# A SwiGLU feed-forward network with seven block products moved from the down projection to the up and gate projections

## The chip, the cores and the metric

The program runs on one core of a Trainium2 chip. Its time is the device time of one execution in microseconds (us); the median of three runs is compared. Five engines work side by side, each through its own queue: TensorE (PE: matrix products into PSUM, with its weight loads shown as PEld), VectorE (DVE), ScalarE (ACT), GpSimd (POOL) and SyncE (SP, which here starts most of the transfers).

## The reference

Two layers act on a state h of 512 tokens by 1024 channels, all in float32. Each layer is an RMSNorm, an input projection into four head groups (two kinds of softmax attention, a gated delta rule and a gated linear attention), an output projection, and then the part that matters here, a feed-forward network of width 2816, followed by a gate from a second input:

```
hn = _rmsnorm(h, norm_ffn[l])
h = h + (jax.nn.silu(hn @ w_gate[l]) * (hn @ w_up[l])) @ w_down[l]
gate = jax.nn.sigmoid(_rmsnorm(h, norm_ple[l]) @ w_ple_gate[l])
h = h + gate * (p[l] @ w_ple_proj[l])
```

`_rmsnorm(x, g)` is x divided by the root of the mean of its squares (plus 1e-6), times g. After the two layers one more RMSNorm follows.

## The kernel before

The state is kept transposed: channels on the 128 partitions, 512 tokens along a row, so h is eight tiles `h[0..7]` of 128x512. Every float32 operand of a product is split into a high and a low part in a narrower float format (`hi` by an ACT copy, `lo` by a DVE subtraction), and each product of a 128x128 weight block with a tile is three matmuls, hi by hi, hi by lo and lo by hi (`mm3`, lines 309 to 311, recorded for every product of the kernel).

A plain block (`block`, `gblock`) makes 128 rows of a projection: it loads eight 128x128 weight blocks in two halves of 128x512 (`weights`, lines 278 to 282, from four raw buffers into four pairs of split buffers), and accumulates eight times three matmuls of 512 columns in one of two `acc` banks of PSUM.

`seven` makes a 2x2 block product by seven block products in place of eight (Strassen's scheme in Winograd's form). The fixed side is a 2x2 arrangement of weights: two row blocks of the output by two halves of the depth, `a11, a21, a22, a12`, each 128 x (128 per pair). The moving side is a 2x2 arrangement of two tiles of depth by two halves of 256 tokens, or sums of these made in advance. Each of the seven products is, with four pairs, twelve matmuls of 256 columns; DVE makes the sums of the weights (lines 392, 393, 397 or 403, 418) and, for each of the seven products, ACT and DVE split the fixed side (`fixed_parts`, lines 362 and 363). Four banks of the pools `mixg` and `mixl` take the results.

The feed-forward network of a layer runs in three parts of 8, 8 and 6 of its 22 blocks f (`FF_PARTS`). In every part, for each f, a plain block of gate, a product with R (the reciprocal root of the norm, line 1428), Silu on ACT, a plain block of up, and two products on DVE (lines 1437 and 1438) make a tile u. In parts 0 and 1 two such tiles go through `moving_parts`, which makes the moving side's sums and splits; then four calls of `seven` make the part's share of the eight rows of down and add it to h, and what several results share is collected in `u2` and added by `shared_sums` after part 1. In part 2 the tiles are split plainly, and eight plain down blocks of six products each are added to h (line 1450). A norm comes before (`norm`, which also makes gate block 0) and after.

The order of the work on each engine is made when the program is built: the framework takes instructions in program order where they are ready by its own estimate and where buffers are free, so an instruction can stand ahead of others that come before it in the text. At run time each engine works through its list in that order, and waits on semaphores. A buffer tag holds a fixed number of tiles (`G_BUFS`, `BIG_BUFS`, `RP_BUFS`); whoever asks for one more waits for the first that is let go.

Of the kernel before, what the change touches and what calls it, by code (L numbers as in the profile page):

```python
# [8 lines left out]
F32 = mybir.dt.float32  # L9
# [22 lines left out]
ACC_BUFS = 2  # L32
BIG_BUFS = 5

M_TAGS = (("g",) * 5 + ("e",) * 2, ("g",) * 5 + ("e",) * 2, ("g",) * 4 + ("lg",) * 2 + ("e",), ("g",) * 3 + ("pt",) * 2 + ("o",) * 2)
RP_BUFS = 4
DEPTH = 2
FF = 2816
# [94 lines left out]
def _weights(i):  # L133

    tiles = {}

    def tblock(key, b):
        k = b.shape[0] // P
        t = np.zeros((P, 8, P), np.float32)
        t[:, :k] = b.reshape(k, P, P).transpose(1, 0, 2)  # L140
        tiles[key] = t.reshape(P, D)

    for l in range(DEPTH):
        w = np.asarray(i["w_in"][l])
# [12 lines left out]
        pp = np.asarray(i["w_ple_proj"][l]).reshape(2, P, 2, 4, P)  # L157
        for half in range(2):
            tiles[l, "ple", half] = pp[:, :, half].transpose(1, 2, 0, 3).reshape(P, D)
        w, wp = np.asarray(i["w_out"][l]), np.asarray(i["w_ple_gate"][l])  # L160
        wa = w[:2 * P].reshape(2, P, 2, 4, P)
        for half in range(2):
            tiles[l, "outa", half] = wa[:, :, half].transpose(1, 2, 0, 3).reshape(P, D)
        g, u, dn = (np.asarray(i[n][l]) for n in ("w_gate", "w_up", "w_down"))
        for n in range(KB):
            c = slice(n * P, (n + 1) * P)
            tblock((l, "out", n), w[2 * P:, c])
            tblock((l, "pgate", n), wp[:, c])
            for part, (f0, nf) in enumerate(FF_PARTS):
                d = dn[f0 * P:(f0 + nf) * P, c]  # L170
                if part < 2:

                    d = d.reshape(nf // 2, 2, P, P).transpose(1, 0, 2, 3).reshape(nf * P, P)
                tblock((l, "down", part * KB + n), d)
        for f in range(FB):
            tblock((l, "gate", f), g[:, f * P:(f + 1) * P])
            tblock((l, "up", f), u[:, f * P:(f + 1) * P])
    return np.stack([tiles[k] for k in _TILES])


# [22 lines left out]
class _Trunk:  # L203
# [122 lines left out]
        return ps  # L326


    def moving_parts(self, u, j):

        nc = self.nc
        t = self.gp.tile([P, 2 * T], F32, tag="rp", bufs=RP_BUFS, name=self.name("t"))
        u4, t4 = (a.rearrange("p (a b c) -> p a b c", a=2, b=2) for a in (u, t))

        nc.vector.tensor_sub(t4[:, :, 0, :], u4[:, :, 1, :], u4[:, 0])
        nc.vector.tensor_sub(t4[:, 0, 1, :], u4[:, 1, 1, :], t4[:, 0, 0, :])
        nc.vector.tensor_sub(t4[:, 1, 1, :], u4[:, 1, 0, :], t4[:, 0, 1, :])
        tags = iter(M_TAGS[j])
        tile = lambda: self.g("m", F32R, tag=next(tags))
        first = tile()  # L340
        b11 = first[:, :256], first[:, 256:]
        nc.scalar.activation(b11[0], u4[:, 0, 0, :], AF.Copy)
        nc.vector.tensor_sub(b11[1], u4[:, 0, 0, :], b11[0].bitcast(F32))
        parts = []
        for src in (t[:, :T], t[:, T:], u[:, T:]):
            hi, lo = tile(), tile()
            nc.scalar.activation(hi, src, AF.Copy)
            nc.vector.tensor_sub(lo, src, hi.bitcast(F32))
            parts += [(hi[:, c:c + 256], lo[:, c:c + 256]) for c in (0, 256)]
        return [b11, *parts]  # L350

    def raw(self, name, i, c, n):
        raw = self.wrp.tile([P, HALF], F32, tag="w", name=self.name("w"))
# [9 lines left out]
        nc.vector.tensor_sub(lo, raw, hi.bitcast(F32))  # L363
        return hi, lo

    def seven(self, ms, name, i, h, u2, part):

        nc = self.nc
        n = len(ms) * P
        a11, a21, a22, a12 = (self.raw(name, part * KB + i + r, c * n, n) for r, c in ((0, 0), (1, 0), (1, 1), (0, 1)))

        def product(ps, parts, which, start=True, pairs=range(len(ms))):
            hi, lo = parts
# [8 lines left out]
        left, right = slice(0, 256), slice(256, 512)  # L385
# [3 lines left out]
        early, late = range(len(ms) - (i == 0)), range(len(ms) - (i == 0), len(ms))  # L389
# [6 lines left out]
        if i == 0:  # L396
# [5 lines left out]
        if i:  # L402
            nc.vector.tensor_sub(a21, a11, a21)
            w7 = self.fixed_parts(a21)
        if part == 0:
            nc.scalar.activation(u2, p1, AF.Copy)
        else:
            nc.vector.tensor_add(u2, u2, p1)
# [4 lines left out]
        nc.vector.tensor_add(h[1][:, right], h[1][:, right], p5)  # L413
        product(p1, self.fixed_parts(a12), b21, start=False)
        nc.vector.tensor_add(h[0][:, left], h[0][:, left], p1)
        product(p7, self.fixed_parts(a22), t4, start=False)
        nc.vector.tensor_add(h[1][:, left], h[1][:, left], p7)
        nc.vector.tensor_sub(s2, a12, s2)
        product(p5, self.fixed_parts(s2), b22, start=False)
        nc.vector.tensor_add(h[0][:, right], h[0][:, right], p5)  # L420

    def shared_sums(self, h, u2):

        nc = self.nc
        nc.vector.tensor_add(h[0][:, 256:], h[0][:, 256:], u2)
        h2 = h[1].rearrange("p (a t) -> p a t", a=2)
        nc.vector.tensor_add(h2, h2, u2.unsqueeze(1).to_broadcast([P, 2, 256]))

    def gvproj(self, xs, name):

# [955 lines left out]
    def run(self):  # L1386
# [11 lines left out]
        for l in range(DEPTH):  # L1398
# [13 lines left out]
            self.gt = "gl"  # L1412
            xs, R, ps = self.norm(h, self.v(V_FFN, KB), "gate")
            self.table("silu_and_others")
            for part, (f0, nf) in enumerate(FF_PARTS):
                if part == 2:
                    ph = []
                    for k in range(2):
                        t = self.g("pt")
                        nc.sync.dma_start(t, self.pT[l, k])  # L1420
                        ph.append(self.split(t, "p"))
                ms = []
                if part == 0:
                    u2 = self.gp.tile([P, KB // 2, 256], F32, tag="rp", bufs=RP_BUFS, name=self.name("u2"))
                for f in range(f0, f0 + nf):
                    pg = self.block(xs, "gate", f) if f else ps
                    t, sg = self.g("fg"), self.g("fs")
                    nc.vector.tensor_mul(t, pg, R)  # L1428
                    self.act(sg, t, AF.Silu)
                    pu = self.block(xs, "up", f)  # L1430
                    if part == 2:
                        u = self.g("fu")
                    elif f % 2 == 0:
                        both = self.big("fu")
                    if part < 2:
                        u = both[:, f % 2 * T:(f % 2 + 1) * T]
                    nc.vector.tensor_mul(u, pu, R)  # L1437
                    nc.vector.tensor_mul(u, u, sg)
                    if part == 2:
                        self.gt = "g"  # L1440
                        ms.append(self.split(u, "m"))
                        self.gt = "gl"
                    elif f % 2:
                        ms.append(self.moving_parts(both, len(ms)))
                for n in range(0, KB, 1 if part == 2 else 2):
                    if part < 2:
                        self.seven(ms, "down", n, h[n:n + 2], u2[:, n // 2, :], part)
                        continue
                    ps = self.block(ms, "down", part * KB + n)
                    nc.vector.tensor_add(h[n], h[n], ps)  # L1450
                if part == 1:
                    for n in range(0, KB, 2):
                        self.shared_sums(h[n:n + 2], u2[:, n // 2, :])

            self.gt = "g"
            self.table("natural_log_exp_and_others")
# [107 lines left out]
```

## Time and profile before

| what | before |
|---|---|
| median of 3 runs | 1516.2 us (1514.39 to 1516.46) |
| the profiled execution's own time | 1513.12 us |
| its span, instructions | 1511.3 us, 27858 |
| PE, PEld busy | 1460.5 us (97%), 1220.8 us (81%) |
| DVE, ACT, POOL busy | 1004.9 us (66%), 681.1 us (45%), 113.8 us (8%) |
| mean granted TensorE clock | 0.983 |

The busy shares are means over stages of different kinds. An operation's duration runs from its start to its end and overlaps its successor's, so the pace of a row of like operations is read from start to start. In the views a group's line is that of the helper that issued it: the tile names (`acc` for a plain block, `bank` for `seven`) tell the stages apart.

### The profile page before, as it was taken

The page shows a single profiled execution, that of the slowest core. Times are in us where ns is not written, and L with a number is a line of the kernel's source. Part 1 is how long each engine was busy: PE and PEld are TensorE (multiplying, and loading weights), DVE is VectorE, ACT ScalarE, POOL GpSimd, SP SyncE. Part 2 cuts the span into 40 slices and gives each one's busy share as a digit, 9 for nine tenths or more (in the row PEclk, how much of TensorE's full clock was granted, in tenths as well). Part 3 has the DMA queues.
Part 4 walks back from the last instruction along what each step waited for, and adds up shares of the span by engine and source line. Part 5 has one row for each costly group of instructions (what it writes and reads, how often), then busy time and mean ns, then how long its engine had stood idle before and what let it go on. Part 6 is the DMA issues. An engine that isn't in the chain of part 4 may idle for free.

```text
span 1511.3 us, 27858 instructions
## 1 busy us (share of the span) xinstructions
PE 1460.5 (97%) x10856; PEld 1220.8 (81%) x10856; DVE 1004.9 (66%) x2012; ACT 681.1 (45%) x1298; POOL 113.8 (8%) x174
## 2 busy tenths in 40 slices
PE   8989999999999999999999899899999999999996
PEld 6768787878898889887878788778788988898875
DVE  7757865666585679456687558565765956874654
ACT  7624533544443434344574434344543434343554
POOL 0151020100000000000003401210000000000011
PEclk9999999999999999999999979999999999999998
DMA  5485125423323324323434721362232333243232
GB/s 200 101 227 109 41 67 173 126 81 99 97 89 113 97 78 133 97 82 112 129 105 108 207 72 49 101 184 74 92 97 90 100 105 98 77 133 95 91 95 77
DMA packets 108631, 162.55 MB, mean 108 GB/s; under 512 B 26803, under 2 KB 36436, under 8 KB 108500
## 3 DMA queue, kind: packets, MB, share of 16 engines
q1 hardware_dynamic: 83328, 142.95, 30.1%
q0 software_dynamic: 7872, 14.68, 4.1%
q10 hardware_dynamic: 17300, 3.14, 1.3%
q8 instruction: 86, 1.41, 0.4%
q14 instruction: 45, 0.37, 0.1%
HBM read 141.72 MB, written 19.01 MB: 106 GB/s over the span
## 4 chain that ended last, share of the span: by engine, by line
PE 84%; DVE 6%; issue 3%; DMA 3%; ACT 2%; POOL 2%; ACTq 0%; DVEq 0%; SPq 0%; POOLq 0%
PE acc L309 21%; PE acc L310 20%; PE acc L311 20%; PE bank L309 3%; PE bank L311 3%; PE bank L310 3%; PE mix L624 2%; PE mix L615 1%; PE mix L593 1%; DMA rp<-qk 1%; PE acc L445 1%; PE acc L443 1%; PE mix L1267 1%; DMA nx<-dn 1%; PE acc L444 1%
## 5 line engine op out<-in xcount | busy, mean ns | idle before, releaser
L309 PE MATMUL acc<-y,wh 128*128 128x512 f32 x1320 | 531.5, 403 | 11.8 <-ACT wh L281 7.6
L311 PE MATMUL acc<-y,wl 128*128 128x512 f32 x1320 | 522.8, 396 | 1.7 <-issue 0.9
L310 PE MATMUL acc<-y,wh 128*128 128x512 f32 x1320 | 521.5, 395 | 0.3 <-DVE y L525 0.3
L281 ACT ACTIVATE wh<-w 128x512 fp32r<-128x512 f32 (+1 forms) x404 | 243.2, 604 | 391.8 <-PE acc L310 315.0
L282 DVE TENSOR_TENSOR wl<-w,wh 128x512 fp32r<-128x512 f32 (+1 forms) x404 | 267.8, 664 | 145.7 <-ACT wh L281 144.7
L309 PEld LDWEIGHTS acc<-y,wh 128*128 128x128 f32 x1320 | 251.1, 190 | 72.0 <-ACT wh L281 9.9
L311 PEld LDWEIGHTS acc<-y,wl 128*128 128x128 f32 x1320 | 250.9, 190 | 56.0 <-issue 2.0
L310 PEld LDWEIGHTS acc<-y,wh 128*128 128x128 f32 x1320 | 251.0, 190 | 50.1 <-DVE y L525 2.1
L309 PE MATMUL bank<-m,wh 128*128 128x256 f32 x448 | 126.8, 286 | 2.7 <-ACT wh L362 2.3
L311 PE MATMUL bank<-m,wl 128*128 128x256 f32 x448 | 126.1, 283 | 0.5 <-DVE wl L363 0.5
L310 PE MATMUL bank<-m,wh 128*128 128x256 f32 x448 | 126.4, 283 | 0.0
L309 PEld LDWEIGHTS bank<-m,wh 128*128 128x128 f32 x448 | 85.2, 192 | 5.4 <-ACT wh L362 3.7
L266 ACT ACTIVATE e<-logit,mx 128x128 f32<-128x128 f32 (+3 forms) x96 | 53.5, 557 | 76.2 <-DVE mx L603 73.9
L311 PEld LDWEIGHTS bank<-m,wl 128*128 128x128 f32 x448 | 85.8, 192 | 0.9 <-DVE wl L363 0.9
L310 PEld LDWEIGHTS bank<-m,wh 128*128 128x128 f32 x448 | 85.9, 192 | 0.4
L1437 DVE TENSOR_TENSOR fu<-acc,rstd 128x512 f32<-128x512 f32 x44 | 30.4, 691 | 61.4 <-PE acc L311 61.4
L1428 DVE TENSOR_TENSOR fg<-acc,rstd 128x512 f32<-128x512 f32 x44 | 30.3, 689 | 49.2 <-PE acc L311 46.1
L362 ACT ACTIVATE wh<-s 128x512 fp32r<-128x512 f32 x48 | 30.1, 628 | 64.7 <-DVE s L393 31.8
L624 PEld LDWEIGHTS mix<-vn,pt 128*128 128x128 f32 x320 | 44.8, 195 | 7.2 <-DVE pt L621 1.9
L362 ACT ACTIVATE wh<-w 128x512 fp32r<-128x512 f32 x64 | 40.1, 630 | 21.4 <-PE bank L310 15.1
L624 PE MATMUL mix<-vn,pt 128*128 128x64 f32 x320 | 45.6, 273 | 0.5 <-DVE pt L621 0.3
L363 DVE TENSOR_TENSOR wl<-w,wh 128x512 fp32r<-128x512 f32 x64 | 43.9, 686 | 2.9 <-ACT wh L362 2.1
(320 smaller groups left out, 2079.3 us busy)
## 6 DMA issues: line engine op xcount, KB each, us to landing
w<-wt SPq DMA_DIRECT2D x420, 256.0 KB, 2.6
rp<-qk POOLq DMA_DIRECT2D x32, 256.0 KB, 5.5
qk<-qkh SPq DMA_DIRECT2D x24, 256.0 KB, 4.8
qk<-qkl SPq DMA_DIRECT2D x24, 256.0 KB, 5.2
rp<-qk POOLq DMA_DIRECT2D x12, 512.0 KB, 4.3
w<-wt SPq DMA_DIRECT2D x48, 128.0 KB, 2.2
h<-xT SPq DMA_DIRECT2D x16, 256.0 KB, 4.7
spill<-h SPq DMA_DIRECT2D x8, 256.0 KB, 3.1
```

The lines of the kernel that those rows point to most:

```text
L266: i = self.nc.scalar.activation(out, in_, func, **k).ins
L281: nc.scalar.activation(hi[:, :n], raw[:, :n], AF.Copy)
L282: nc.vector.tensor_sub(lo[:, :n], raw[:, :n], hi[:, :n].bitcast(F32))
L309: nc.tensor.matmul(ps, wh, xh, start=start, stop=False, **how)
L310: nc.tensor.matmul(ps, wh, xl, start=False, stop=False, **how)
L311: nc.tensor.matmul(ps, wl, xh, start=False, stop=stop, **how)
L362: nc.scalar.activation(hi, raw, AF.Copy)
L363: nc.vector.tensor_sub(lo, raw, hi.bitcast(F32))
L443: nc.tensor.matmul(o, xh[:, tok], hi, start=first, stop=False, skip_group_check=True)
L624: nc.tensor.matmul(po, pt[:, kb * P:(kb + 1) * P], v(kb), start=kb == 0, stop=kb == qb, skip_group_check=True)
L1428: nc.vector.tensor_mul(t, pg, R)
L1437: nc.vector.tensor_mul(u, pu, R)
```

## The change

Gate, up and down swap their forms. Up is made by `seven` for all pairs of blocks f but the first (ten units a layer), gate by `seven` for the pairs 8, 10, 12, 14, 16 and 18 (six units); gate pairs 0 to 6 and 20, and up pair 0, stay plain. All of down is made of plain blocks, with the splits of u that these need. The moving side of the new units comes from h itself: `normed_parts` scales four pairs of tiles of h by the gain on ACT, forms the sums on DVE and splits them, once a layer, after the first pair. The plain down blocks of a part no longer stand behind it but in the next part, between its gate and up units: none beside pair 8, then two behind up 8, then one ahead of and one behind each up; in part 2 none beside pair 16, four behind up 16, two ahead of and two behind up 18. The down blocks of part 2 still come last. The results go out through `scaled` (gate, times R) and `gated` (up, times the gate's tile, which is silu(g R) times R). `moving_parts`, `u2` and `shared_sums` are gone.

```diff
+GATES = range(8, 20, 2)
-    def moving_parts(self, u, j):
...
+    def differences(self, u0, u1):
+        a, b = slice(0, 256), slice(256, 512)
+        nc.vector.tensor_sub(u0[:, a], u0[:, b], u0[:, a])
+        nc.vector.tensor_sub(u0[:, b], u1[:, b], u0[:, b])
+        nc.vector.tensor_sub(u1[:, b], u1[:, b], u0[:, a])
+        nc.vector.tensor_sub(u1[:, a], u1[:, a], u1[:, b])
+    def normed_parts(self, h, gain, xs, j):
+        us = [self.g("x", tag="g") for _ in range(2)]
+        for u, x, c in zip(us, h, range(2)):
+            nc.scalar.activation(u, x, AF.Copy, scale=gain[:, c:c + 1])
+        self.differences(*us)
...
+            out += self.parts_of(u, hi, lo)
...
-    def seven(self, ms, name, i, h, u2, part):
+    def seven(self, ms, name, i, take, late_rows=False):
...
-        nc.vector.tensor_add(u2, u2, p6)
-        product(p7, w7, t3, pairs=late if i == 0 else early)
-        nc.vector.tensor_add(h[1][:, right], h[1][:, right], p7)
+        take("1", p1)
+        take("6", p6)
+        product(p7, w7, t3, pairs=late if late_rows else early)
+        take("7", p7)
...
+    def gated(self, u, gates):
+        u2 = self.g("u2", tag="gl")[:, :256]
+        q = [u[:, c:c + 256] for c in range(0, 1024, 256)]
+        def take(what, ps):
+            if what == "1":
+                nc.scalar.activation(u2, ps, AF.Copy)
+            elif what == "6":
+                nc.vector.tensor_add(u2, u2, ps)
+            elif what == "7":
+                nc.vector.tensor_add(q[3], u2, ps)
+            elif what == "5":
+                nc.vector.tensor_add(q[3], q[3], ps)
+            elif what == "11":
+                nc.vector.tensor_mul(q[0], ps, gates[0][:, :256])
+            elif what == "21":
+                nc.vector.tensor_add(q[2], u2, ps)
+                nc.vector.tensor_mul(u[:, T:], u[:, T:], gates[1])
+            else:
+                nc.vector.tensor_add(q[1], u2, ps)
+                nc.vector.tensor_mul(q[1], q[1], gates[0][:, 256:])
...
             for part, (f0, nf) in enumerate(FF_PARTS):
+                split, made = made, []
+                downs = list(range(KB)) if part else []
+                per = 2 if part == 2 else 1
+                for f in range(f0, f0 + nf, 2):
+                    if part == 2 and not downs:
...
+                    if f in GATES:
+                        self.seven(xts, "gate", f, self.scaled(gates, R))
+                    for j, t in enumerate(gates):
+                        if f not in GATES:
+                            nc.vector.tensor_mul(t, self.block(xs, "gate", f + j) if f + j else ps, R)
+                        self.act(t, t, AF.Silu)
+                        nc.vector.tensor_mul(t, t, R)
+                        if f == 0:
+                            nc.vector.tensor_mul(us[j], self.block(xs, "up", j), t)
+                    if split:
+                        ms = [self.split(m[:, c:c + T], "m") for m in split for c in (0, T)]
+                        split = []
+                    elif downs:
+                        for n in downs[:per]:
+                            down(n)
+                        downs = downs[per:]
+                    if f == 0:
+                        xts = [self.normed_parts(h[2 * j:2 * j + 2], self.v(V_FFN + 2 * j, 2), xs[2 * j:2 * j + 2], j)
+                               for j in range(KB // 2)]
+                    else:
+                        self.seven(xts, "up", f, self.gated(both, gates))
+                    made.append(both)
+                    n2 = per + per * (f == f0)
+                    for n in downs[:n2]:
+                        down(n)
+                    downs = downs[n2:]
+            ms += [self.split(m[:, c:c + T], "m") for m in made for c in (0, T)]
+            for n in range(KB):
+                acc = self.block(ms, "down", 2 * KB + n)
+                nc.vector.tensor_add(h[n], h[n], acc)
```

`scaled` is built as `gated` is, with R in place of the gate's tile and one product on 512 columns and two on 256. The order of the weights in memory follows the new forms; their amount is the same.

## Rows read from the trace of the kernel before

**Rows 1.** The page: busy engines, and the chain that ended last by engine.
```profile
PE 1460.5 (97%) x10856; PEld 1220.8 (81%) x10856; DVE 1004.9 (66%) x2012; ACT 681.1 (45%) x1298; POOL 113.8 (8%) x174
...
PE 84%; DVE 6%; issue 3%; DMA 3%; ACT 2%; POOL 2%; ACTq 0%; DVEq 0%; SPq 0%; POOLq 0%
```
**Rows 2.** Windows, layer 0's feed-forward: us, PE, PEld, DVE, ACT, POOL, clock, DMA, GB/s.
```profile
341.00:363.00 22.00, 22.00 (x95) 17.53 (x95) 13.71 (x23) 9.40 (x15) 0.00 (x0) 1.00 0.35 108
363.00:426.70 63.70, 63.70 (x283) 52.76 (x282) 39.24 (x65) 24.93 (x41) 0.00 (x0) 1.00 0.29 91
426.70:467.20 40.50, 40.12 (x327) 39.35 (x326) 37.20 (x70) 19.26 (x35) 0.00 (x0) 1.00 0.32 100
467.20:557.80 90.60, 90.60 (x416) 75.63 (x415) 52.59 (x87) 33.63 (x56) 0.00 (x0) 1.00 0.32 98
557.80:600.00 42.20, 40.97 (x328) 39.84 (x327) 41.37 (x83) 19.21 (x33) 0.00 (x0) 1.00 0.36 111
655.00:688.00 33.00, 33.00 (x147) 27.33 (x146) 20.78 (x34) 17.12 (x30) 0.00 (x0) 1.00 0.31 92
```
**Rows 3.** Timeline of PE, plain blocks: start, duration, engine, line, operation.
```profile
639.61 0.39 PE L309 MATMUL acc<-y,wh 128*128 128x512 f32 x1
639.84 0.39 PE L310 MATMUL acc<-y,wh 128*128 128x512 f32 x1
...
647.09 0.39 PE L309 MATMUL acc<-y,wh 128*128 128x512 f32 x1
```
**Rows 4.** Timeline of PE, inside a unit of seven products.
```profile
449.72 0.28 PE L309 MATMUL bank<-m,wh 128*128 128x256 f32 x1
449.84 0.28 PE L310 MATMUL bank<-m,wh 128*128 128x256 f32 x1
...
452.96 0.28 PE L309 MATMUL bank<-m,wh 128*128 128x256 f32 x1
```
**Rows 5.** Groups by line between 340 and 690 us, with what ended the idle time.
```profile
L309 PE MATMUL bank<-m,wh 128*128 128x256 f32 x224 | 63.4, 286 | 1.3 <-ACT wh L362 1.1
...
L281 ACT ACTIVATE wh<-w 128x512 fp32r<-128x512 f32 (+1 forms) x101 | 62.1, 615 | 112.2 <-PE acc L310 101.0 <-PE bank L310 4.0 <-ACT sq L508 2.9
```
**Rows 6.** Timeline of PE: first matmul of four units, and first behind them.
```profile
426.69 0.28 PE L309 MATMUL bank<-m,wh 128*128 128x256 f32 x1
...
468.44 0.40 PE L309 MATMUL acc<-y,wh 128*128 128x512 f32 x1
...
555.51 0.28 PE L309 MATMUL bank<-m,wh 128*128 128x256 f32 x1
...
598.11 0.40 PE L309 MATMUL acc<-y,wh 128*128 128x512 f32 x1
...
1170.66 0.28 PE L309 MATMUL bank<-m,wh 128*128 128x256 f32 x1
...
1212.40 0.40 PE L309 MATMUL acc<-y,wh 128*128 128x512 f32 x1
...
1299.46 0.28 PE L309 MATMUL bank<-m,wh 128*128 128x256 f32 x1
...
1342.06 0.40 PE L309 MATMUL acc<-y,wh 128*128 128x512 f32 x1
```
**Rows 7.** Timeline of PE, its longest wait in a unit.
```profile
567.92 0.28 PE L311 MATMUL bank<-m,wl 128*128 128x256 f32 x1
568.84 0.39 PE L309 MATMUL bank<-m,wh 128*128 128x256 f32 x1 [0.64 <-ACT wh L362]
```
**Rows 8.** Timeline of DVE inside the units of part 1.
```profile
589.26 0.68 DVE L363 TENSOR_TENSOR wl<-w,wh 128x512 fp32r<-128x512 f32 x1
589.86 0.41 DVE L408 TENSOR_TENSOR u<-u,bank 128x256 f32<-128x256 f32 x1
590.19 0.68 DVE L363 TENSOR_TENSOR wl<-s,wh 128x512 fp32r<-128x512 f32 x1
590.80 0.68 DVE L363 TENSOR_TENSOR wl<-w,wh 128x512 fp32r<-128x512 f32 x1
```
**Rows 9.** Windows of about one unit each, late in part 1 and in part 0.
```profile
578.00:588.00 10.00, 10.00 (x85) 10.00 (x85) 9.74 (x21) 3.75 (x7) 0.00 (x0) 1.00 0.40 133
588.00:598.00 10.00, 10.00 (x86) 10.00 (x85) 9.87 (x21) 5.80 (x10) 0.00 (x0) 1.00 0.42 132
456.00:466.00 10.00, 10.00 (x86) 10.00 (x85) 8.96 (x18) 5.06 (x9) 0.00 (x0) 1.00 0.33 105
```

More of the change, by code (lines that the diff above doesn't have):

```diff
@@ L169, in _weights @@
             for part, (f0, nf) in enumerate(FF_PARTS):
[L170 to L174, printed above, removed]
+                tblock((l, "down", part * KB + n), dn[f0 * P:(f0 + nf) * P, c])
         for f in range(FB):
-            tblock((l, "gate", f), g[:, f * P:(f + 1) * P])
-            tblock((l, "up", f), u[:, f * P:(f + 1) * P])
+            pairs = lambda d: d.reshape(KB // 2, 2, P, P).transpose(1, 0, 2, 3).reshape(D, P)
+            c = slice(f * P, (f + 1) * P)
+            tblock((l, "gate", f), pairs(g[:, c]) if f // 2 * 2 in GATES else g[:, c])
+            tblock((l, "up", f), pairs(u[:, c]) if f > 1 else u[:, c])
     return np.stack([tiles[k] for k in _TILES])
@@ L326, in gblock @@
         return ps
-    def moving_parts(self, u, j):
+    def differences(self, u0, u1):
         nc = self.nc
[L332 to L350, printed above, removed]
+        a, b = slice(0, 256), slice(256, 512)
[3 more added lines that the diff above has]
+        nc.vector.tensor_sub(u1[:, a], u1[:, a], u1[:, b])
@@ new lines, in parts_of @@
+    def parts_of(self, src, hi, lo):
+        nc = self.nc
+        nc.scalar.activation(hi, src, AF.Copy)
+        nc.vector.tensor_sub(lo, src, hi.bitcast(F32))
+        return [(hi[:, c:c + 256], lo[:, c:c + 256]) for c in range(0, src.shape[1], 256)]
+    def normed_parts(self, h, gain, xs, j):
+        nc = self.nc
+        us = [self.g("x", tag="g") for _ in range(2)]
+        for u, x, c in zip(us, h, range(2)):
+            nc.scalar.activation(u, x, AF.Copy, scale=gain[:, c:c + 1])
+        self.differences(*us)
+        tags = iter(X_TAGS[j])
+        out = []
+        for u in us:
+            tag = next(tags)
+            if tag == "rp":
+                p = self.gp.tile([P, 2, T], F32R, tag="rp", bufs=RP_BUFS, name=self.name("xt"))
+                hi, lo = p[:, 0, :], p[:, 1, :]
+            else:
+                hi, lo = self.g("xt", F32R, tag=tag), self.g("xt", F32R, tag=next(tags))
+            out += self.parts_of(u, hi, lo)
+        t1, t3, t4, t2 = out
+        cut = lambda k, c: tuple(x[:, c:c + 256] for x in xs[k])
+        return [cut(0, 0), t1, t2, t3, t4, cut(1, 0), cut(1, 256)]
@@ L364, in fixed_parts @@
         return hi, lo
-    def seven(self, ms, name, i, h, u2, part):
+    def seven(self, ms, name, i, take, late_rows=False):
         nc = self.nc
         n = len(ms) * P
-        a11, a21, a22, a12 = (self.raw(name, part * KB + i + r, c * n, n) for r, c in ((0, 0), (1, 0), (1, 1), (0, 1)))
+        a11, a21, a22, a12 = (self.raw(name, i + r, c * n, n) for r, c in ((0, 0), (1, 0), (1, 1), (0, 1)))
         def product(ps, parts, which, start=True, pairs=range(len(ms))):
@@ L384, in seven @@
         b11, t1, t2, t3, t4, b21, b22 = range(7)
-        left, right = slice(0, 256), slice(256, 512)
         p1, p6, p7, p5 = (bank(t) for t in ("mixg", "mixl", "mixg", "mixl"))
         s1, s2 = (self.g(s, tag="gl")[:, :n] for s in ("s1", "s2"))
-        early, late = range(len(ms) - (i == 0)), range(len(ms) - (i == 0), len(ms))
+        early, late = range(len(ms) - late_rows), range(len(ms) - late_rows, len(ms))
         w1 = self.fixed_parts(a11)
@@ L401, in seven @@
         product(p6, w6, t2, pairs=late)
-        if i:
+        if not late_rows:
             nc.vector.tensor_sub(a21, a11, a21)
             w7 = self.fixed_parts(a21)
[L405 to L408, printed above, removed]
-        nc.vector.tensor_add(u2, u2, p6)
-        product(p7, w7, t3, pairs=late if i == 0 else early)
-        nc.vector.tensor_add(h[1][:, right], h[1][:, right], p7)
+        take("1", p1)
@@ L412, in seven @@
+        take("6", p6)
+        product(p7, w7, t3, pairs=late if late_rows else early)
+        take("7", p7)
         product(p5, self.fixed_parts(s1), t1)
-        nc.vector.tensor_add(h[1][:, right], h[1][:, right], p5)
+        take("5", p5)
         product(p1, self.fixed_parts(a12), b21, start=False)
-        nc.vector.tensor_add(h[0][:, left], h[0][:, left], p1)
+        take("11", p1)
         product(p7, self.fixed_parts(a22), t4, start=False)
-        nc.vector.tensor_add(h[1][:, left], h[1][:, left], p7)
+        take("21", p7)
@@ new lines, in gated, with take @@
+    def gated(self, u, gates):
+        nc = self.nc
+        u2 = self.g("u2", tag="gl")[:, :256]
+        q = [u[:, c:c + 256] for c in range(0, 1024, 256)]
+        def take(what, ps):
+            if what == "1":
+                nc.scalar.activation(u2, ps, AF.Copy)
+            elif what == "6":
+                nc.vector.tensor_add(u2, u2, ps)
+            elif what == "7":
+                nc.vector.tensor_add(q[3], u2, ps)
+            elif what == "5":
+                nc.vector.tensor_add(q[3], q[3], ps)
+            elif what == "11":
+                nc.vector.tensor_mul(q[0], ps, gates[0][:, :256])
+            elif what == "21":
+                nc.vector.tensor_add(q[2], u2, ps)
+                nc.vector.tensor_mul(u[:, T:], u[:, T:], gates[1])
+            else:
+                nc.vector.tensor_add(q[1], u2, ps)
+                nc.vector.tensor_mul(q[1], q[1], gates[0][:, 256:])
+        return take
@@ L1414, in run, with down @@
             self.table("silu_and_others")
+            made, ms, downs = [], [], []
+            def down(n):
+                acc = self.block(ms, "down", (part - 1) * KB + n)
+                nc.vector.tensor_add(h[n], h[n], acc)
             for part, (f0, nf) in enumerate(FF_PARTS):
[L1416 to L1439, printed above, removed]
-                        self.gt = "g"
-                        ms.append(self.split(u, "m"))
-                        self.gt = "gl"
-                    elif f % 2:
-                        ms.append(self.moving_parts(both, len(ms)))
@@ L1445, in run @@
[L1445 to L1453, printed above, removed]
+                split, made = made, []
@@ new lines, in run @@
+                downs = list(range(KB)) if part else []
+                per = 2 if part == 2 else 1
+                for f in range(f0, f0 + nf, 2):
+                    if part == 2 and not downs:
+                        self.gt = "g"
+                        ph = []
+                        for k in range(2):
+                            t = self.g("pt", tag="gl")
+                            nc.sync.dma_start(t, self.pT[l, k])
+                            ph.append(self.split(t, "p"))
+                        ms = [self.split(m[:, c:c + T], "m") for m in made for c in (0, T)]
+                        self.gt = "gl"
+                        made = []
+                    both = self.big("fu")
+                    us = both[:, :T], both[:, T:]
+                    gates = [self.g("fg") for _ in range(2)]
+                    if f in GATES:
[8 more added lines that the diff above has]
+                    if split:
+                        self.gt = "g"
+                        ms = [self.split(m[:, c:c + T], "m") for m in split for c in (0, T)]
+                        self.gt = "gl"
+                        split = []
[6 more added lines that the diff above has]
+                               for j in range(KB // 2)]
+                    else:
+                        self.seven(xts, "up", f, self.gated(both, gates))
[4 more added lines that the diff above has]
+                    downs = downs[n2:]
```

23 lines of the change are left out of this document (16 added, 7 removed).

## Prediction

> **What bounds the kernel now.** I read the page first: PE is busy for 97% of the span and carries 84% of the chain that ended last [rows 1]. Then the windows, to see whether that holds where the change is: in layer 0's feed-forward, from 341 to 688 us, PE is busy in whole windows of plain blocks to the last hundredth while DVE works 39.24 of 63.70 us [rows 2]; only the two stretches of seven block products leave PE idle, 0.38 us of 40.50 and 1.23 us of 42.20, and there DVE is busy nearly throughout. The clock is 1.00 in every one of these windows, the upper of the two levels, and the DMA share is about a third. So in this stage the end is set by how many matmuls PE issues and at what pace, with DVE as the next engine in line inside the units.
>
> The pace comes from the timeline, start to start. Plain: 33 matmuls between 639.61 and 647.09, so 0.2267 us each of 512 columns [rows 3]. Units: 27 between 449.72 and 452.96, so 0.120 us each of 256 columns [rows 4], a little over half.
>
> **What the change removes and adds on PE.** A plain pair of blocks of eight products is 48 matmuls, 48 x 0.2267 = 10.88 us; a unit with four pairs of depth is 7 x 12 = 84 matmuls, 84 x 0.120 = 10.08 us. Each unit in place of a plain pair gains 0.80 us. Before, a layer has 8 units (the 224 matmuls of each of three lines, 672 in all, of [rows 5]); after, 16: ten for up, six for gate. Per layer: gate and up lose 32 plain blocks, 768 matmuls, down gains 16, 384 matmuls, so 384 fewer of 512 columns (87.05 us) and 672 more of 256 (80.64 us). That is 6.41 us a layer, 12.8 us in two.
>
> **Waits that go.** Four units in a row should take 336 x 0.120 = 40.32 us. From the first matmul to the first behind the last they take 41.75, 42.60, 41.74 and 42.60 us in the four parts [rows 6], so 1.43 + 2.28 + 1.42 + 2.28 = 7.4 us is lost in waits. The longest is 568.84, where PE stands for the ACT and DVE splits of a fixed side [rows 7], just behind the last `moving_parts`; the last units of part 1 run with no wait although DVE is busy 9.74 and 9.87 of 10 us [rows 9]. So it is not the load of a unit that costs, but the backlog that a batch of other DVE work leaves as units begin. All four of these stretches go.
>
> **DVE, which could take PE's place.** Back to back, an operation of 512 columns takes 0.60 us of DVE and one of 256 columns 0.33 us [rows 8]. An old unit is 7 splits, 4 sums of weights and 6 or 7 additions of 256: 8.6 to 8.9 us, and with its share of `shared_sums` in part 1 9.8 us. A new one is the same 11 x 0.60, seven operations of 256 and one of 512: 6.6 + 2.3 + 0.6 = 9.5 us, against 10.08 us of PE. Per pair in part 1, with silu times R twice: 2 x 9.5 + 1.2 = 20.2 us against 20.16; a plain down block is two splits and an addition, 1.8 us against 5.44 of PE. So a pair with two down blocks is 23.8 us of DVE in 31.0 us of PE. It fits, but between two down blocks DVE has nothing to spare, and it can be ahead only by the four split buffers: ACT waits 101.0 of its 112.2 us in the plain blocks for PE to give one back [rows 5]. ACT in a unit is seven splits and a copy, and 5.80 of 10 us is the most in the windows [rows 9]; it isn't next.
>
> **New waits, per layer.** (a) The moving side. `normed_parts` issues 16 DVE operations of 256 and 8 of 512, 16 x 0.33 + 8 x 0.60 = 10.1 us, and 16 on ACT, needed at up 2. They can start as soon as h is final, beside the first blocks, where DVE is idle for 22.00 - 13.71 = 8.3 us [rows 2]; the rest, 1.8 us, competes with the splits for gate 2 and 3, which stand behind it in the program. From below 0; from above 4 us, twice the rest, as ACT and DVE alternate. I take 1.0. (b) The eight splits of u in the middle of pairs 8 and 16: 8 x 0.60 = 4.8 us of DVE each time between two units, with no down block beside them; queued behind them are the splits of up's weights, and PE waits for those. From below 0, if the early tiles are split before; from above 4.8 each, all of it bare. The nearest rows are the batches ahead of units in the kernel before, 1.43 and 2.28 us; I take their mean, 1.85, twice: 3.7. (c) The other fourteen units: from 0, as the last units of part 1 have, to 0.57 us each (2.28 / 4); the nearest rows are units amid units, so 0.07 each, 1.0 in all. The sum is 5.7 us a layer, 11.4 in two.
>
> What else moves costs nothing on this path: the weights' bytes are the same and come over the same queue with the DMA share at 0.32 in a stretch of units [rows 2]; the 48 loads of a part stand in another order on SP, four for a unit as for two plain blocks. In the last plain down blocks of part 2 the two newest tiles of u are used last, in the fifth and sixth product of each block, so their splits have 12 matmuls to hide behind, as before.
>
> **The sum.** -12.8 (PE's matmuls) - 7.4 (old waits) + 11.4 (new waits) = -8.8 us. The profiled execution took 1513.12 us, so 1504.3; it lies 3.1 us under the median of the runs, and I set the change on the median: 1507.4, rounded to 1507.
>
> A page speaks against all of this. The Trainium skill (TensorE: Matmul & The Clock Gate, section Back-to-back issue gap) gives sustained spacings of about 81 ns at 128 columns and 131 ns at 512, by which wide matmuls are far cheaper by the column; on the straight line between, an estimate, 256 columns cost 98 ns, and the sum of matmuls would be 2 x (672 x 0.098 - 384 x 0.131) = +31 us. This trace has 227 and 120 ns, and the measurement decides.
>
> **Rivals.** (1) All new waits hide: the early tiles are split in idle moments and the x parts beside block 0. For it speaks the slack of DVE in plain blocks; against it, that four of four earlier batches cost something. -12.8 - 7.4 = -20.2: 1496. Chance 0.13.
>
> (2) Nothing gained: the sixteen splits in the middle of pairs 8 and 16 lie bare, 9.6 us a layer. For it, that DVE is full in the units on both sides; against it, that six of eight tiles are ready long before. -20.2 + 19.2 = -1.0: 1515. Chance 0.12.
>
> (3) Slower: DVE cannot catch up between units. Its list is in fixed order, and a result that it must take from a bank, waiting for PE, holds the splits that PE needs next. At 0.57 us for every one of the 16 units (the price of part 1 before), with (a) and (b) as taken: 9.1 + 1.0 + 3.7 = 13.8 us a layer, 27.6 in two, -20.2 + 27.6 = +7.4: 1524. It decides from 10.1 us of waits a layer on. For it: 20.2 us of DVE against 20.16 of PE in a pair. Against it: 9.87 of 10 us was carried without a wait [rows 9], and down blocks give 3.6 us of slack each. Chance 0.13.
>
> (4) Slower by the page's rule: 256 columns cost more of PE in gate and up than in down. Break-even, with waits alike, is 87.05 / 672 = 0.1295 us a matmul; the slowest stretch of units, waits included, had 42.60 / 336 = 0.127 [rows 6], and the operands are of one shape and type. At 0.1295, with the waits as taken, the time would be 1516.2 + 11.4 - 7.4 = 1520. Chance 0.02.
>
> **Chances.** The forecast, between 1499 and 1513, has 0.60; with (1) that is 0.73 for faster by over 0.2% (3 us, about what a measurement of this kernel tells from no change), 0.12 for within 0.2%, 0.15 for slower. The range: with no wait 1496, so 1497 at the low end; at the high end it takes in (2) and a part of (3), up to 1518, where waits are 11 us a layer.
>
> **What would show it.** Matmuls of 256 columns into `bank`: 896 on each of three lines in place of 448, at 0.120 us start to start, and 2 x 384 fewer of 512 columns. The feed-forward of a layer shorter by 4 us. Waits of PE for the splits at the start of up 8 and up 16, about 2 us each, and little at gate 2. The prediction is wrong if the pace is not 0.120, if PE's waits pass 10 us a layer, or if they vanish.

## The result, and the profile after

The changed kernel is slower: 1523.2 us median against 1511.9 us (15 runs of each), a ratio of 1.0073 with a 95% interval of 1.0053 to 1.0092, so about 11 us. The forecast was 1507 us, faster: 8.8 us under the 1516.2 us that the first three runs of the kernel before had given. One run in the experiments below, 4917 us of the kernel with plain up blocks, is left out of its ratio. The page of the changed kernel answers to [rows 1]: PE does less (1452.8 us of matmuls for 1460.5) in a longer span, DVE more, and DVE's share of the chain that ended last goes from 6% to 11%.

```profile
span 1526.8 us, 29321 instructions
...
PE 1452.8 (95%) x11432; PEld 1241.3 (81%) x11432; DVE 1096.1 (72%) x2196; ACT 717.0 (47%) x1370; POOL 115.7 (8%) x174
...
PE 78%; DVE 11%; DMA 4%; issue 3%; ACT 2%; POOL 2%; ACTq 0%; DVEq 0%; SPq 0%; POOLq 0%
```

The stage of the change can be timed by itself: from the last matmul of the norm's sum ahead of the feed-forward to the same matmul of the next norm. That is the windows' first column here (us, PE, PEld, DVE, ACT, POOL, clock, DMA, GB/s), the whole stage of layer 0 first, then the stretch before pair 2's up unit, then that unit:

```profile
343.62:704.54 360.92, 350.61 (x2148) 315.42 (x2147) 279.48 (x495) 160.25 (x272) 0.00 (x0) 0.99 0.32 97
358.70:368.78 10.08, 10.08 (x47) 8.33 (x46) 4.68 (x8) 1.90 (x3) 0.00 (x0) 1.00 0.29 90
368.78:382.70 13.92, 11.94 (x85) 11.53 (x84) 11.67 (x21) 6.47 (x11) 0.00 (x0) 0.88 0.34 98
```

The stage took 354.31 and 354.29 us in the two layers before, and 360.92 and 361.08 after: +13.4 us in two. In both kernels it repeats to 0.2 us between the two layers of the profiled execution, while the stages around it differ by several us from one execution to the next, so below it is the finer measure and the ratio of whole runs the test of it.

A unit of 84 matmuls is 10.08 us at 0.120 us each; pair 2's takes 13.92 us. Measured so (the time from a unit's first matmul to the first behind it, less 0.120 for each of its matmuls), the waits in layer 0 are:

| units | waits, us |
|---|---|
| up 2, behind plain gate blocks | 3.85 |
| up 4, behind plain gate blocks | 2.49 |
| up 6, behind plain gate blocks; then gate 8 and up 8 | 2.50; 0; 1.4 |
| gate 16 and up 16 | 0; 1.5 |
| up 20, behind plain gate blocks | 4.14 |
| the eight others (pairs 10, 12, 14 and 18) | 0 |

That is 15.9 us, and 16.0 in layer 1. Thirteen of it is in the four units that come straight behind plain gate blocks. Not all of that is standing still: in up 2 and up 20, in both layers, PE also ran at half its clock for a while, which is about 1.4 us of the 3.85 (the last section has the rows). What PE stands for there is seen in its timeline at up 2 (start, duration, engine, line; in brackets the idle time and what ended it): the first product runs through, and the second is late by 1.40 us and again by 0.58, for the splits of the second fixed side.

```profile
370.09 0.28 PE L312 MATMUL bank<-y,wl 128*128 128x256 f32 x1
371.77 0.39 PE L310 MATMUL bank<-xt,wh 128*128 128x256 f32 x1 [1.40 <-ACT wh L376]
371.99 0.28 PE L311 MATMUL bank<-xt,wh 128*128 128x256 f32 x1
372.85 0.58 PE L312 MATMUL bank<-xt,wl 128*128 128x256 f32 x1 [0.58 <-DVE wl L377]
373.23 0.41 PE L310 MATMUL bank<-xt,wh 128*128 128x256 f32 x1
```

Why they are late is in DVE's timeline. Line 1500 is the product of a plain gate block with R, 1502 the product of its Silu with R, 405 and 406 the sums of weights s1 and s2 that the second fixed side is made of.

```profile
363.54 0.69 DVE L1500 TENSOR_TENSOR fg<-acc,rstd 128x512 f32<-128x512 f32 x1 [1.54 <-PE acc L312]
364.93 0.69 DVE L1502 TENSOR_TENSOR fg<-fg,rstd 128x512 f32<-128x512 f32 x1 [0.70 <-ACT fg L267]
368.98 0.69 DVE L1500 TENSOR_TENSOR fg<-acc,rstd 128x512 f32<-128x512 f32 x1 [3.35 <-PE acc L312]
369.58 0.68 DVE L405 TENSOR_TENSOR s<-w,w 128x512 f32<-128x512 f32 x1
370.30 0.69 DVE L406 TENSOR_TENSOR s<-s,w 128x512 f32<-128x512 f32 x1
370.91 0.68 DVE L1502 TENSOR_TENSOR fg<-fg,rstd 128x512 f32<-128x512 f32 x1
371.51 0.69 DVE L416 TENSOR_TENSOR w<-w,w 128x512 f32<-128x512 f32 x1
372.11 0.68 DVE L377 TENSOR_TENSOR wl<-s,wh 128x512 fp32r<-128x512 f32 x1
```

DVE is idle for 3.35 us before 368.98: the second product with R stands at the head of its list and waits for PE to end the second gate block. s1 stands right behind it. Its weights had been asked for at 357.19 to 360.49,

```profile
357.19 3.30 SPq L368 DMA_DIRECT2D w<-wt  x4
```

and with the 2.9 us that such a load takes to land (median) they were there by about 363.4, six us before they were used. So when PE ends the gate block and starts the unit, the chain of s1, s2, an ACT split and a DVE split is still to come, and the first product's 1.44 us can't cover it.

### The profile page after: what moved, and what is told of

Same layout as the page of the kernel before. It is cut to its first block, busy times and chain, and to the rows that moved or that the text cites. A ratio compares the mean times of both kernels' runs of the same rounds, so it can differ in the third digit from the quotient of the medians.

```text
span 1526.8 us, 29321 instructions
## 1 busy us (share of the span) xinstructions
PE 1452.8 (95%) x11432; PEld 1241.3 (81%) x11432; DVE 1096.1 (72%) x2196; ACT 717.0 (47%) x1370; POOL 115.7 (8%) x174
## 4 chain that ended last, share of the span: by engine, by line
PE 78%; DVE 11%; DMA 4%; issue 3%; ACT 2%; POOL 2%; ACTq 0%; DVEq 0%; SPq 0%; POOLq 0%
PE acc L310 16%; PE acc L311 15%; PE acc L312 15%; PE bank L312 6%; PE bank L310 6%; PE bank L311 6%; PE mix L680 2%; DVE wl L377 1%; PE mix L671 1%; DMA u<-du 1%; DMA nx<-dn 1%; PE acc L501 1%; DMA rp<-qk 1%; PE acc L499 1%; DVE wl L283 1%
## 5 line engine op out<-in xcount | busy, mean ns | idle before, releaser
L310 PE MATMUL acc<-y,wh 128*128 128x512 f32 x808 | 331.8, 411 | 13.4 <-ACT wh L282 8.0
L311 PE MATMUL acc<-y,wh 128*128 128x512 f32 x808 | 321.7, 398 | 0.5 <-DVE y L581 0.5
L312 PE MATMUL acc<-y,wl 128*128 128x512 f32 x808 | 321.0, 397 | 0.8 <-DVE wl L283 0.8
L310 PEld LDWEIGHTS acc<-y,wh 128*128 128x128 f32 x808 | 153.9, 191 | 53.3 <-ACT wh L282 10.4
L311 PEld LDWEIGHTS acc<-y,wh 128*128 128x128 f32 x808 | 154.3, 191 | 31.2 <-DVE y L581 2.7
L310 PE MATMUL bank<-xt,wh 128*128 128x256 f32 x512 | 149.2, 291 | 15.6 <-ACT wh L376 15.5
L312 PE MATMUL bank<-xt,wl 128*128 128x256 f32 x512 | 148.2, 291 | 3.9 <-DVE wl L377 3.9
L311 PE MATMUL bank<-xt,wh 128*128 128x256 f32 x512 | 147.4, 288 | 0.0
L311 PE MATMUL acc<-ml,wh 128*128 128x512 f32 x352 | 137.4, 390 | 0.0
L310 PE MATMUL acc<-mh,wh 128*128 128x512 f32 x352 | 137.2, 390 | 0.0
L312 PE MATMUL acc<-mh,wl 128*128 128x512 f32 x352 | 137.0, 389 | 0.0
L311 PE MATMUL bank<-y,wh 128*128 128x256 f32 x384 | 108.7, 283 | 0.0
L312 PE MATMUL bank<-y,wl 128*128 128x256 f32 x384 | 108.6, 283 | 0.0
L310 PE MATMUL bank<-y,wh 128*128 128x256 f32 x384 | 108.5, 283 | 0.0
```

Source lines behind the costliest of these rows:

```text
L310: nc.tensor.matmul(ps, wh, xh, start=start, stop=False, **how)
L311: nc.tensor.matmul(ps, wh, xl, start=False, stop=False, **how)
L312: nc.tensor.matmul(ps, wl, xh, start=False, stop=stop, **how)
```

## The experiments

Three theories were set against each other. O: the order on DVE's list, as above. C: DVE has too much to do around the units, in whatever order. D: the unit's weights land too late.

**The preparation ahead.** `seven` was cut so that its loads, its sums s1 and s2 and the splits of its first two products can stand ahead of the second gate block:

```diff
         w1 = self.fixed_parts(a11)
-        product(p1, w1, b11, pairs=early)
+        if not first:
+            product(p1, w1, b11, pairs=early)
         nc.vector.tensor_add(s1, a21, a22)
         nc.vector.tensor_sub(s2, s1, a11)
         w6 = self.fixed_parts(s2)
+        if first:
+            yield
+            product(p1, w1, b11, pairs=early)
...
+                        if f and f not in GATES and j:
+                            self.ahead = self.weights("gate", f + j)
+                            unit = self.gseven(xts, "up", f, self.gated(both, gates), first=True)
+                            next(unit)
...
+                    elif unit:
+                        _last(unit)
```

> The changed kernel, but in the pairs 2, 4, 6 and 20 (plain gate, then a unit for up) the up unit's loads, its first sums of weights and the splits of its first two products stand in the program ahead of the second gate block. Nothing is left out. Theory O (order): in the changed kernel DVE's list has the first sum s1 behind the product of the second gate block with R, which waits for PE to end that block, so PE waits 3.9, 2.5, 2.5 and 4.1 us in these four units, 13.0 us a layer; with the sums ahead these waits fall under 1 us each, 18 to 26 us less than the changed kernel, a ratio to the kernel before of 0.990 to 0.996. Rival C (DVE has too much to do in the units, whatever the order): the same DVE work, so within 3 us of the changed kernel, ratio 1.005 to 1.009. Rival D (the unit's weights land too late): loads start no earlier, so the waits stay, ratio 1.005 to 1.009.

Measured: ratio to the kernel before 0.9911 (0.9878 to 0.9943, 12 runs), and 346.74 us for the stage in place of 360.92. The four waits are gone, and the half clock with them; 1.5 us at up 16 and 0.2 at up 8 are left. On DVE the sums now stand behind the first product with R (here line 1514), and the whole preparation fits in the time in which DVE stood idle:

```profile
366.06 0.69 DVE L1514 TENSOR_TENSOR fg<-acc,rstd 128x512 f32<-128x512 f32 x1 [1.54 <-PE acc L312]
366.67 0.68 DVE L410 TENSOR_TENSOR s<-w,w 128x512 f32<-128x512 f32 x1
367.38 0.69 DVE L411 TENSOR_TENSOR s<-s,w 128x512 f32<-128x512 f32 x1
...
369.20 0.69 DVE L377 TENSOR_TENSOR wl<-s,wh 128x512 fp32r<-128x512 f32 x1
...
371.50 0.69 DVE L1514 TENSOR_TENSOR fg<-acc,rstd 128x512 f32<-128x512 f32 x1 [0.29 <-PE acc L312]
```

DVE still waits for PE there, 0.29 us, but with nothing behind it that PE needs. The matmuls, DVE's work (280.31 us, 279.48 before the edit) and the loads (asked for 11.6 us before the unit's first matmul in both) are as in the changed kernel, so C and D fall as explanations of these four waits.

```profile
346.14:692.88 346.74, 345.37 (x2148) 312.08 (x2147) 280.31 (x495) 160.87 (x272) 0.00 (x0) 1.00 0.32 101
```

**The wait alone taken away.** Nothing is moved in the program; the second product with R reads another tile:

```diff
-                            nc.vector.tensor_mul(t, self.block(xs, "gate", f + j) if f + j else ps, R)
+                            pg = self.block(xs, "gate", f + j) if f + j else ps
+                            nc.vector.tensor_mul(t, gates[0] if f and j else pg, R)
```

> The changed kernel with one operand changed: in the pairs 2, 4, 6 and 20 the product of the second gate block with R reads the first block's tile in place of the second block's bank, so that it has nothing to wait for. It leaves out the use of the second gate block's result (its matmuls run); program order and amount of work are as in the changed kernel. From one norm's sum to the next the feed-forward took 361.0 us a layer in the changed kernel and 354.3 before. Theory O: it is the wait of this one instruction that holds s1, so the waits of 13.0 us a layer in the four units fall under 1 us each and the stage takes 347 to 350 us. Rival C (DVE's load) and rival D (late loads): nothing of either is changed, 358 to 361 us.

Measured: 347.21 and 347.02 us in the two layers (one run, 1506.1 us). s1 stands behind the same instruction as in the changed kernel, but 371.22 is now 2.5 us ahead of the unit's first matmul at 373.7, where it was 0.8 us behind it, and the four waits are gone (up 8 waits 0.7 us, up 16 its 1.5). C and D fall here without anything moved.

```profile
369.88 0.69 DVE L1503 TENSOR_TENSOR fg<-fg,rstd 128x512 f32<-128x512 f32 x1 [0.70 <-ACT fg L267]
370.61 0.69 DVE L1501 TENSOR_TENSOR fg<-fg,rstd 128x512 f32<-128x512 f32 x1
371.22 0.69 DVE L405 TENSOR_TENSOR s<-w,w 128x512 f32<-128x512 f32 x1
```

**Only the sums ahead.** As the first experiment, with `fixed_parts` of the first two products behind the second gate block in the program.

```diff
+        if first:
+            nc.vector.tensor_add(s1, a21, a22)
+            nc.vector.tensor_sub(s2, s1, a11)
+            yield
         w1 = self.fixed_parts(a11)
...
```

> As the kernel with the preparation ahead (346.7 us a layer), but only the loads and the two sums of weights stand ahead of the second gate block, and the splits of the first two products behind it. Nothing is left out. Theory O: the sums are what stood behind the wait, and the splits follow where they are ready: 346 to 348 us a layer. Rival: the splits too have to be ahead, two on ACT and two on DVE of about 0.6 us each, so 1 to 2.5 us of wait stay in each of the four units: 351 to 357 us.

Measured: 346.81 and 346.68 us (one run, 1491.2 us). The two sums are enough; the splits follow by themselves.

**No unit behind a plain gate block.** Up is plain in pairs 2, 4, 6 and 20.

```diff
-                        if f == 0:
-                            nc.vector.tensor_mul(us[j], self.block(xs, "up", j), t)
+                        if f not in GATES:
+                            nc.vector.tensor_mul(us[j], self.block(xs, "up", f + j), t)
...
-                    else:
+                    elif f in GATES:
                         self.seven(xts, "up", f, self.gated(both, gates))
```

> The changed kernel with plain up blocks in the pairs 2, 4, 6 and 20, so 12 units a layer in place of 16 and none behind a plain gate block. Nothing is left out. Theory O: 4 x 0.80 us a layer given up, +6.4 us in two, and the 13.0 us of waits a layer gone, -26: together about -20 us against the changed kernel, ratio to before 0.992 to 0.998. Rival C: the twelve units left stand closest together and have the most DVE work, so waits stay in them; a gain of less than 6 us, ratio 1.003 or more.

Measured: ratio 0.9921 (0.9891 to 0.9951, 8 runs), 349.60 us. That is 2.9 us a layer above the preparation ahead, where 4 x 0.80 = 3.2 are given up. Up 8 waits 0.1 us here: its 1.4 us in the changed kernel were for the most part the lateness of up 6 handed on. Not wholly: with the wait alone taken away up 6 is in time and up 8 still waits 0.7 us.

**Units for gate in all pairs from 2 on.**

```diff
-GATES = range(8, 20, 2)
+GATES = range(2, 22, 2)
```

> The changed kernel with units for gate in all pairs from 2 to 20, so 20 units a layer and no plain gate block ahead of a unit; in part 0 there are no plain blocks between units at all. Nothing is left out. Theory O: 4 x 0.80 us a layer more gained, -6.4 us in two; the 13.0 us of waits a layer go, and each new pair of units waits as pairs 8 and 16 do now, 1.4 us, 5.6 us a layer: together about -21 us against the changed kernel, ratio to before 0.991 to 0.998. Rival C: pairs 2 to 8 are eight units in a row with 20.2 us of DVE in 20.16 us of PE and no slack, so the waits grow along them and the gain is under 5 us, or a loss: ratio 1.004 or more.

Measured: ratio 0.9942 (0.9920 to 0.9964, 10 runs), 353.95 and 353.55 us. The run of eight units from gate 2 to up 8 waits 10.6 us, 1.3 each, and DVE is busy for 84.54 of its 87 us. Three windows of that stretch, and last a unit behind a plain down block, which has none of this:

```profile
358.00:368.80 10.80, 9.79 (x76) 9.20 (x75) 10.80 (x20) 4.78 (x10) 0.00 (x0) 1.00 0.30 97
390.00:400.00 10.00, 9.17 (x73) 8.62 (x72) 10.00 (x20) 4.36 (x8) 0.00 (x0) 1.00 0.20 64
433.00:445.00 12.00, 11.19 (x91) 10.79 (x90) 12.00 (x24) 6.04 (x11) 0.00 (x0) 1.00 0.31 104
460.90:471.00 10.10, 10.10 (x86) 10.09 (x85) 7.67 (x14) 4.78 (x9) 0.00 (x0) 1.00 0.35 114
```

So theory C is true, but of another kernel: without plain blocks between them units are bound by DVE. My expectation had these waits wrong (5.6 us a layer in all). It had the total right only by chance: in the stage the gain on the changed kernel is 7.0 and 7.5 us a layer, where 10.6 was expected, and against the kernel before it is 0.4 and 0.7 us, while whole runs are some 9 us shorter. Most of that difference lies outside the stage, and no run here shows why.

**The splits of u behind the up unit.**

```diff
-                    if split:
-                        self.gt = "g"
-                        ms = [self.split(m[:, c:c + T], "m") for m in split for c in (0, T)]
-                        self.gt = "gl"
-                        split = []
-                    elif downs:
+                    if not split:
...
+                    if split:
+                        self.gt = "g"
+                        ms = [self.split(m[:, c:c + T], "m") for m in split for c in (0, T)]
+                        self.gt = "gl"
+                        split = []
                     made.append(both)
```

> The changed kernel with the splits of u in the middle of pairs 8 and 16 moved behind the up unit. Nothing is left out. Theory of the prediction (b): these splits are what makes PE wait 1.4 and 1.5 us in the up units 8 and 16; 2 to 6 us less than the changed kernel. Theory O: most of the splits are done long before, and the waits come from the gate unit's last results and the two products with R, which stand ahead of the up unit's third split on DVE; no change within 3 us, and the waits of 1.4 and 1.5 us stay.

Measured: ratio 1.0074 (1.0049 to 1.0100, 9 runs), 361.07 and 362.25 us, and 1.6 us of wait in up 16. (The two layers differ by 1.2 us here as the clock fell to half in two of the four units in layer 0 and in three in layer 1.) This tells nothing on the splits of pair 16: though they had been moved in the program, seven of the eight still ran on DVE in the 13 us ahead of up 16, as in the changed kernel. That the list puts them there because the tiles they write come free only then is likely, and not shown.

**Gate plain in pair 16, with the preparation ahead.**

```diff
-GATES = range(8, 20, 2)
+GATES = (8, 10, 12, 14, 18)
```

> The preparation ahead, and gate plain in pair 16: 15 units a layer, with 10.9 us of plain blocks where the eight splits of u stand. Nothing is left out. Theory of the prediction (b): the wait of 1.5 us in up 16, there in all five kernels that have this pair, is that of the splits without a plain block beside them; it goes, one unit's 0.80 us is given up: 346.0 us a layer. Rival: the wait belongs to up 16 itself (its loads or its banks) and stays: 347.5 us.

Measured: 346.12 and 345.97 us (one run, 1497.2 us), and no wait in up 16. Its 1.5 us is what the eight splits cost in a pair of units without a plain block. A gate unit straight ahead does not do it alone: with the preparation ahead up 8 has one too, with only two of its eight splits in it, and waits 0.2 us. So the theory given for the last experiment, that the gate unit's own results make up 16 wait, was wrong.

**The best version.** The preparation ahead, and `GATES = (4, *range(8, 22, 2))`.

> The preparation ahead, and units for gate also in pairs 4 and 20: 18 units a layer. Nothing is left out. Two units more are 2 x 0.80 us a layer. Theory O with slack: pair 20 waits 0.1 us as in the kernel with units for gate in all pairs, and pair 4 has plain blocks on both sides, so 345.3 us a layer and a ratio to the kernel before of 0.986 to 0.990. Rival C: the eight units without plain blocks between them waited 10.4 us, 1.3 us each; if pair 4 waits so in both its units, 347.5 us or more, and the ratio is that of the preparation alone, 0.991.

Measured: ratio 0.9900 (0.9877 to 0.9922, 6 runs), 345.38 and 345.37 us a layer; pair 4 waits 0.2 us in the three units from up 2 on, pair 20 0.1. It beats both kernels. From the preparation alone it can't be told by whole runs; the stage is 1.36 us a layer shorter, where 2 x 0.80 less these waits was expected.

```profile
350.99:696.37 345.38, 344.02 (x2220) 314.35 (x2219) 290.99 (x521) 164.01 (x280) 0.00 (x0) 1.00 0.32 102
```

## Why the prediction was wrong

**PE's matmuls: right.** 896 matmuls of 256 columns on each of three lines into `bank` (512 + 384 by their moving side), and inside a unit without waits 0.120 us each. With the preparation ahead the stage is 7.6 us a layer shorter than before, and the term is needed in full for that: 6.4 from it and 3.7 from the old waits, less the 1.7 us left in up 8 and up 16 and 0.7 at the third plain block (below), make 7.7. The sustained spacings that the prediction takes from the Trainium skill (TensorE: Matmul & The Clock Gate, section Back-to-back issue gap), by which this term would, as an estimate, have been a loss of 31 us, have nothing for them here: the trace has 0.227 and 0.120 us.

**The old waits: right.** They went with the units in down, 3.7 us a layer.

**New waits, (a) and (b): near.** (a) PE waits for nothing at gate 2; 1.0 us was forecast. (b) 1.5 us at up 16, for 1.85, and 1.4 at up 8, for the other 1.85; but there it is 0.1 to 0.7 once up 6 is in time, so that half of the term was near by luck.

**New waits, (c): this step failed.** "The other fourteen units: from 0 ... to 0.57 us each (2.28 / 4); the nearest rows are units amid units, so 0.07 each, 1.0 in all." The row taken was that of a unit behind a unit (and 0.07 is no row's value: the third and fourth units of a stretch before wait 0, the second 0.51 and 1.26). Ten of the fourteen are like it, or stand behind plain down blocks, and wait 0. Four stand behind plain gate blocks, and these took 13.0 us a layer, 3.2 each, over five times the upper bound. Some 3 us of the 13.0 is the half clock in up 2 and up 20 (an estimate: 3.85 and 4.14 less the 2.5 of up 4 and up 6), for which the prediction had no term: the clock had been 1.00 in all its rows. One of its own signs of being wrong came true with this: PE's waits passed 10 us a layer. Set into the sum, -12.8 - 7.4 + 31.9 = +11.7 us, against +13.4 in the stage and about +11 in the runs. Of the 0.9 us a layer that is left, 0.7 is a wait at the third plain block of the stage, for a bank that the first product with R gives back; the kernel before does not have it.

The trace of the kernel before showed the order that did it, and the prediction did not look there. There too s1 (line 392) stood right behind the product of the pair's second gate block with R (line 1428), which waits for PE, and was let go with it at 422.06:

```profile
421.45 0.69 DVE L1428 TENSOR_TENSOR fg<-acc,rstd 128x512 f32<-128x512 f32 x1 [1.54 <-PE acc L311]
422.06 0.68 DVE L392 TENSOR_TENSOR s<-w,w 128x512 f32<-128x512 f32 x1
422.78 0.69 DVE L393 TENSOR_TENSOR s<-s,w 128x512 f32<-128x512 f32 x1
```

The unit came at 426.69 [rows 6], a plain up block later, and these 4.6 us were the cover. The change takes that block away and puts the unit directly behind the gate block. A plain down block in front of a unit does no harm, though its addition to h needs PE's result as well: nine such units have no wait. On DVE's list s1 and s2 stand ahead of that addition there, and s1 runs 3.8 to 9.3 us before the unit starts. Gate 10, which starts at 462.12 in the changed kernel (line 1476 is the addition):

```profile
454.44 0.69 DVE L405 TENSOR_TENSOR s<-w,w 128x512 f32<-128x512 f32 x1 [1.31 <-DMA w<-wt]
...
456.25 0.69 DVE L406 TENSOR_TENSOR s<-s,w 128x512 f32<-128x512 f32 x1
...
462.31 0.69 DVE L1476 TENSOR_TENSOR h<-h,acc 128x512 f32<-128x512 f32 x1 [1.54 <-PE acc L312]
```

**The rivals.** The third had the time, 1524, and half the mechanism: a fixed list on which a result to be taken from a bank holds the splits that PE needs. It gave the loss to all sixteen units and to DVE's load, and both are wrong for this kernel: most of the loss is in four, and DVE stood idle for 3.35 us ahead of each. So its time was met by luck: 0.57 us in each of sixteen units, set on a base of 1516.2, in place of 3.2 in four, on 1511.9. It had 0.13; the slack that down blocks give was no argument against it where no down block stands.

What stays open is why s1 was put behind an instruction that was ready later: the list is made from the framework's own estimates when the program is built, and the trace shows only what came of it.

## What to carry to other kernels

When two kinds of work change places, look in the trace of before at what stands on each helper engine's list between the last instruction that waits for the bottleneck and the first that feeds it, and ask whether the new neighbour leaves time for that chain. A cost taken from "the nearest row" has to be taken from the same pair of neighbours. A busy share says little here: DVE was at 72%, and idle exactly where PE needed it, and moving two sums ahead of one wait, in four units, was worth 14 us a layer.

## What the runs showed of the hardware

In two of the four units behind plain gate blocks PE came back from its waits at half its clock. In up 2 the granted clock from 373 to 376 us was 0.51, the lower of the two levels, and the matmuls of 256 columns started 0.21 us apart. In up 20 it was 0.50 for 3.41 us. In up 4, behind waits of the same 1.40 and 0.58 us, it stayed at 1.00. The rows are two stretches of up 2 and the same two of up 4, as far behind the unit's first matmul, then up 20, and last the whole units up 2 and up 4:

```profile
370.00:373.00 3.00, 1.02 (x7) 0.61 (x5) 2.93 (x6) 2.06 (x5) 0.00 (x0) 0.92 0.00 0
373.00:376.00 3.00, 3.00 (x15) 3.00 (x16) 2.33 (x5) 1.59 (x3) 0.00 (x0) 0.51 0.50 165
394.83:397.83 3.00, 1.02 (x7) 0.61 (x6) 2.93 (x6) 2.06 (x5) 0.00 (x0) 1.00 0.00 0
397.83:400.83 3.00, 3.00 (x26) 3.00 (x27) 2.87 (x6) 1.93 (x4) 0.00 (x0) 1.00 0.51 167
655.85:659.26 3.41, 3.33 (x15) 3.33 (x16) 2.71 (x6) 1.76 (x4) 0.00 (x0) 0.50 0.37 115
368.78:382.70 13.92, 11.94 (x85) 11.53 (x84) 11.67 (x21) 6.47 (x11) 0.00 (x0) 0.88 0.34 98
393.61:406.18 12.57, 10.59 (x85) 10.18 (x84) 11.59 (x21) 6.48 (x11) 0.00 (x0) 1.00 0.37 109
```

In the stretch in which the clock fell, PE did the same work in both units, busy for 1.02 of 3 us. Both units leave PE idle for 1.98 us; the slower clock is the whole difference between the 3.85 us of up 2 and the 2.49 of up 4, 1.4 us. Which units it hits can differ between the two layers of one execution: in the kernel with the splits of u behind the up unit it fell in up 2 and up 6 in layer 0, and in up 2, up 4 and up 20 in layer 1. What decided is not settled by these runs. In the stages without these waits, before the change and with the preparation ahead, the clock stayed at 1.00, so part of what a wait of 2 us costs here is paid after it.
